# Attention tables by query tile, an own tile for the latent keys, and a Hyena front loaded and evacuated in another order

## The chip, the cores and the metric

The kernel runs on one core of a Trainium2 chip. The metric is the device time of one execution in microseconds (us). The core has a matrix engine (TensorE, PE in the profile, with its weight loads as PEld), VectorE (DVE), ScalarE (ACT), GpSimd (POOL) and SyncE (SP, which here only issues DMAs). Each engine works through its own instructions in order; semaphores tie them together. ScalarE, GpSimd and SyncE each issue DMAs from their own queue.

## The reference

Two layers of an encoder over 512 tokens of width 1024, batch 1, in float32:

```python
for layer in range(2):
    h = rms_norm(x, mix_pre_norm[layer])
    m = even_mixer(h, ...) if layer == 0 else odd_mixer(h, ...)
    x = x + rms_norm(m, mix_post_norm[layer])
    h = rms_norm(x, ffn_pre_norm[layer])
    f = (gelu(dwconv3(h @ w_gate, conv_w)) * (h @ w_up)) @ w_down      # width 2816
    x = x + rms_norm(f, ffn_post_norm[layer])
# even mixer: one projection -> 8 latent attention heads (keys of all heads share a rotated
#   part k_rope of 32) beside 8 neighbourhood heads on an 8 x 64 grid, window 8 x 16:
s = q_row . k_win * scale + rpb[:, row_off, col_off];  p = softmax(s);  o = p . v_win
# odd mixer: one projection -> 4 retention heads (q, k, v, gate) beside 512 Hyena channels:
z = dwconv3(u_proj, short_conv);  x0, x1, v = split(z);  u = v * x1
h_f, h_b = sine_mlp(t) * window                    # the filters, from 33 position features
y = irfft(rfft(u, 1024) * rfft(circ(h_f, h_b)))[:512] + u * hy_bias;  out = y * x0
# both mixers: concat of the two halves, then one output projection
```

## The kernel before, in words

Activations stand transposed: the width of 1024 as eight tiles of 128 partitions, with the 512 tokens along the free dimension. Every float32 product is made of three fp32r products (high x high, low x high, high x low), the `mm` of lines 280 to 282, so a projection of 1024 onto 128 outputs is 24 TensorE instructions with 512 columns ("128x512"). An operand is split by a ScalarE cast (the high part, line 274) and a subtraction of VectorE or GpSimd (the low part, line 275): `split_to`. Weights come as 198 pieces of 512 KB on SyncE's queue; ScalarE casts `whi` (line 259), VectorE subtracts `wlo` (line 260), and pieces are started three ahead. A scheduler in the framework orders each engine's instructions by priorities that the code sets (`high_priority`) and by fixed constraints (`issue_after`). PSUM, eight banks, is shared by tags: pj 2, A 3, B 2, C 1.

The stages, in the profile's time: norm of the input and first projections up to 50 us; neighbourhood heads, with pieces of the latent projections between them, up to about 135; latent heads up to about 250, the output projection; a boundary; the first channel mixer from about 290 to 640, and in its course the making of the Hyena filters (`filters`); a boundary; the second mixer from about 671 to 930; a boundary, and the second channel mixer.

Neighbourhood heads (`na0`, `na1`, `na2`, run in a software pipeline): 128 queries at a time look at a window of 256 keys. There are three kinds of query tile (left edge, middle, right edge). The table of relative positions `rpb` comes as one tile of 8 x 384 values per partition, in four DMAs on SyncE's queue, and the mask `namask` in another; for each head VectorE adds mask and a shifted piece of the table for each kind (line 631). The scores are scaled and biased (line 649), the largest is taken (652), ScalarE takes exponentials (660), the quotient is made (665) and turned by TensorE (671).

Latent attention: `latent_kv` makes the rotated part `kr` of the keys on VectorE and GpSimd (lines 729 to 731). `parts()`, in a later step of the pipeline, splits it three times into `kall` (three pairs of high and low parts, for three heads at a time), a tile that takes over the memory of `rpb` by the shared tag "big". The latent scores are products of `kall` with `qh` and `ql`.

A boundary ends a stage: norm, residual sum, next pre-norm. TensorE meanwhile makes four products of the next stage from the tokens before their row factor is known (`proj_halves`). The factor `rcol` is made by GpSimd (line 299), turned by TensorE (`spread`, line 316, a PSUM buffer of tag C, of which there is one) and copied by ScalarE to `Rb` (line 447); each evacuation then multiplies by it.

Second mixer: at the start ScalarE issues eight DMAs that spill x to memory, and GpSimd two for the forward transform matrices `dftfhi` and `dftflo` (line 934). `conv` evacuates four products, one after another, with the three-point convolution behind each. `spectrum` transforms the filters: their tiles `sd` are loaded by ScalarE's queue, split into `t`, and multiplied in PSUM of tag C; the first half goes to `sp` (line 1027). The signal `u` is made, turned (line 1101), transformed, multiplied by the filter's spectrum (the products `t`, split), and transformed back with `dftihi` and `dftilo`, in PSUM of tag A; the retention's token projections (`proj_tok`, giving `rv`) and three of its gates (`gate`) lie between. `decays` makes the retention's decay factors from eight numbers, 30 small instructions, before the retention.

Of the kernel before, what the change touches and what calls it, by code (L numbers as in the profile page):

```python
# [43 lines left out]
def shape_constants():  # L44
# [18 lines left out]

    mask = np.zeros((P, 3, 32, GR), np.float32)
    for typ, (q0, k0) in enumerate(((0, 0), (16, 8), (48, 32))):
        for p in range(P):
            col = q0 + p // GR
            st = min(max(col - 8, 0), GW - 16)
            kc = k0 + np.arange(32)
            mask[p, typ, (kc < st) | (kc >= st + 16), :] = -1.0e30  # L70
    c["namask"] = f32(mask.reshape(P, 3 * 256))
# [41 lines left out]
def lay_out(inp):  # L113
# [92 lines left out]
class Body:  # L206
    def __init__(self, ctx, tc, I, out, dbg=None):
# [10 lines left out]
        self.filt = self.dp.tile([2, S, HC], F32, name="filt")  # L218
        self.n = 0
        self.wi = 0  # L220
        self.wq = []
        self.cols = self.cp.tile([P, NCOL], F32, name="cols")
# [27 lines left out]
    def load_weight(self, n=1):  # L250
# [88 lines left out]
    def boundary(self, pool, tag, x, prod, gpost, gpre, ns, ftag, perm=False, rin=None):  # L339
# [218 lines left out]
    def mixer0(self, p, h, acc):  # L558
        nc = self.nc
        mask = p.tile([P, 3 * 256], F32, name="namask")  # L560
        rope = p.tile([P, 2, S], F32, name="rope0")
        big = p.tile([P, MH, 384], F32, tag="big", name="rpb")

        def loads():
            nc.sync.dma_start(mask, self.I["namask"])
            for hd in range(0, MH, 2):
                nc.sync.dma_start(big[:, hd:hd + 2], self.I["rpb"][:, hd * 384:hd * 384 + 768].rearrange("p (a b) -> p a b", a=2))
            nc.sync.dma_start(rope, self.I["rope0"].rearrange("p (a b) -> p a b", a=2))
# [53 lines left out]
        def na0(hd, _):  # L622
# [674 lines left out]
```

## Time and profile before

| | |
|---|---|
| time, median of 3 runs | 1312.72 us (1308.06, 1312.72, 1312.88) |
| profiled execution, its own time | 1307.53 us |
| its span | 1305.8 us, 16380 instructions |
| TensorE busy | 1271.7 us, 97% of the span |
| VectorE, ScalarE, GpSimd busy | 813.9, 582.9 and 80.9 us |
| granted TensorE clock, mean | 0.993 of full speed |
| DMA | 130.62 MB, mean 100 GB/s |

The profile is of one execution. A row of the timeline gives the start, the duration, the engine, the line of the kernel, the operation, output and inputs by the program's names, tile sizes, and in brackets how long the engine had been idle before and what it waited for. Matmuls are pipelined, so the spacing of their starts, not the duration of one, is the rate. In a table of stretches, "22.29 (x99)" is 22.29 us of busy time in 99 instructions, and the clock is the mean share of full speed that was granted.

### The profile page before, as it was taken

What the parts mean: (1) busy time and instruction counts of PE and PEld (TensorE: products, weight loads), DVE (VectorE), ACT (ScalarE), POOL (GpSimd) and SP (SyncE); (2) the same over time, 40 slices, a digit from 0 to 9 for tenths busy, and PEclk for the clock granted to TensorE, in tenths of its full rate; (3) what the DMA queues carried; (4) which work ended last, traced back from release to release, by engine and by line L of the source; (5) the groups of instructions that cost most, each with busy time, mean ns of one, the idle gap of its engine ahead of it and who ended that gap; (6) DMA issues with size and microseconds to landing.
All of it is one profiled execution on the core that took longest, in us unless ns stands there. A gap on an engine that the chain in (4) does not pass through costs nothing.

```text
span 1305.8 us, 16380 instructions
## 1 busy us (share of the span) xinstructions
PE 1271.7 (97%) x6370; PEld 1057.5 (81%) x6370; DVE 813.9 (62%) x1298; ACT 582.9 (45%) x943; POOL 80.9 (6%) x73
## 2 busy tenths in 40 slices
PE   9999799999999999999999999999999999999997
PEld 7788677997888788888987878778988888888886
DVE  6679898478766665322588785774875555552223
ACT  5456798456533333222454245544653333332221
POOL 4021322000000000000000000000000000000002
PEclk9999899999999999999999989999999999999999
DMA  7222012223434333333264233214233333333331
GB/s 269 86 65 79 3 33 68 82 79 116 121 123 135 122 113 97 99 111 97 83 226 128 58 120 95 81 49 130 66 113 98 97 97 97 97 97 104 107 97 65
DMA packets 41563, 130.62 MB, mean 100 GB/s; under 512 B 4652, under 2 KB 6892, under 8 KB 40973
## 3 DMA queue, kind: packets, MB, share of 16 engines
q1 hardware_dynamic: 35868, 116.92, 29.0%
q10 hardware_dynamic: 5040, 8.45, 2.0%
q0 software_dynamic: 576, 4.19, 0.9%
q8 instruction: 50, 0.82, 0.3%
q14 instruction: 29, 0.23, 0.1%
HBM read 123.26 MB, written 6.29 MB: 99 GB/s over the span
## 4 chain that ended last, share of the span: by engine, by line
PE 87%; DVE 5%; ACT 3%; issue 2%; DMA 1%; POOL 1%; SPq 0%; DVEq 0%; POOLq 0%; ACTq 0%
PE pspj L280 17%; PE pspj L282 17%; PE pspj L281 17%; PE psA L280 10%; PE psA L282 10%; PE psA L281 10%; DVE wlo L260 1%; ACT e L794 1%; DMA raw<-in_w 1%; PE psB L292 1%; PE psB L671 1%; PE psB L810 1%; DVE h L334 1%; ACT whi L259 1%; PE psC L282 1%
## 5 line engine op out<-in xcount | busy, mean ns | idle before, releaser
L259 ACT CAST whi<-raw 128x1024 fp32r<-128x1024 f32 (+1 forms) x200 | 209.1, 1048 | 432.1 <-PE pspj L281 237.8
L260 DVE TENSOR_TENSOR wlo<-raw,whi 128x1024 fp32r<-128x1024 f32 (+1 forms) x200 | 246.6, 1235 | 204.8 <-ACT whi L259 202.8
L280 PE MATMUL pspj<-h,whi 128*128 128x512 f32 (+1 forms) x664 | 250.5, 377 | 2.8 <-DVE v L599 2.7
L281 PE MATMUL pspj<-h,whi 128*128 128x512 f32 (+1 forms) x664 | 249.6, 376 | 0.0
L282 PE MATMUL pspj<-h,wlo 128*128 128x512 f32 (+1 forms) x664 | 249.4, 376 | 0.0
L282 PE MATMUL psA<-h,wlo 128*128 128x512 f32 (+1 forms) x424 | 155.4, 367 | 0.7 <-DVE wlo L260 0.7
L280 PE MATMUL psA<-h,whi 128*128 128x512 f32 (+1 forms) x424 | 156.1, 368 | 0.0
L281 PE MATMUL psA<-h,whi 128*128 128x512 f32 (+1 forms) x424 | 155.1, 366 | 0.0
L280 PEld LDWEIGHTS pspj<-h,whi 128*128 128x128 f32 x664 | 125.5, 189 | 25.4 <-DVE v L599 3.1
L282 PEld LDWEIGHTS pspj<-h,wlo 128*128 128x128 f32 x664 | 125.4, 189 | 22.2
L281 PEld LDWEIGHTS pspj<-h,whi 128*128 128x128 f32 x664 | 125.5, 189 | 22.0
L280 PE MATMUL pspj<-ahi,whi 128*128 128x512 f32 x308 | 121.4, 394 | 0.0
L282 PE MATMUL pspj<-ahi,wlo 128*128 128x512 f32 x308 | 120.7, 392 | 0.0
L281 PE MATMUL pspj<-alo,whi 128*128 128x512 f32 x308 | 119.5, 388 | 0.0
L282 PEld LDWEIGHTS psA<-h,wlo 128*128 128x128 f32 x424 | 79.8, 189 | 15.5 <-DVE wlo L260 1.9
L280 PEld LDWEIGHTS psA<-h,whi 128*128 128x128 f32 x424 | 80.0, 189 | 14.8 <-issue 2.6
L281 PEld LDWEIGHTS psA<-h,whi 128*128 128x128 f32 x424 | 80.0, 189 | 12.4
L894 DVE TENSOR_TENSOR t<-psA,Rb 128x512 f32<-128x512 f32 x40 | 27.6, 691 | 83.4 <-PE psA L282 83.3
L282 PEld LDWEIGHTS pspj<-ahi,wlo 128*128 128x128 f32 x308 | 57.8, 188 | 13.5
L281 PEld LDWEIGHTS pspj<-alo,whi 128*128 128x128 f32 x308 | 57.8, 188 | 12.9
L280 PEld LDWEIGHTS pspj<-ahi,whi 128*128 128x128 f32 x308 | 57.9, 188 | 11.5
L299 POOL TENSOR_TENSOR r<-v,mhalf 128x2 f32<-128x2 f32 (+1 forms) x14 | 13.7, 977 | 847.7 <-DVE v L297 690.2
(360 smaller groups left out, 2140.1 us busy)
## 6 DMA issues: line engine op xcount, KB each, us to landing
raw<-in_w SPq DMA_DIRECT2D x198, 512.0 KB, 3.5
x<-in_xT SPq DMA_DIRECT2D x16, 256.0 KB, 4.8
fflt<-in_fwin SPq DMA_DIRECT2D x8, 256.0 KB, 2.9
xspill<-f ACTq DMA_DIRECT2D x8, 256.0 KB, 2.6
sd<-filt ACTq DMA_DIRECT2D x8, 256.0 KB, 3.3
x<-xspill ACTq DMA_DIRECT2D x8, 256.0 KB, 3.2
rpb<-in_rpb SPq DMA_DIRECT2D x4, 384.0 KB, 4.6
filt<-fs SPq DMA_DIRECT2D x4, 256.0 KB, 2.5
```

The source lines that it names most:

```text
L259: nc.scalar.copy(hi[:, c], raw[:, c])
L260: nc.vector.tensor_tensor(lo[:, c], raw[:, c], hi[:, c].bitcast(F32), ALU.subtract)
L280: nc.tensor.matmul(ps, stat[0], mov[0], start=start, stop=False)
L281: nc.tensor.matmul(ps, stat[0], mov[1], start=False, stop=False)
L282: self.last_mm = nc.tensor.matmul(ps, stat[1], mov[0], start=False, stop=stop).ins
L292: nc.tensor.matmul(ps[:, j:j + 1], a[:, j * P:(j + 1) * P], self.ones, start=a is accs[0], stop=a is accs[-1])
L299: self.pow = nc.gpsimd.tensor_tensor(r, v, self.mhalf[:, :c], ALU.pow)
L334: self.nc.vector.scalar_tensor_tensor(lo, src, g, hi.bitcast(F32), ALU.mult, ALU.subtract)
L671: tr = lambda o, i: nc.tensor.transpose(o, i, self.ident)
L794: nc.scalar.activation(e, ps, AF.Exp, bias=nmx, accum_out=den[:, i:i + 1])
L810: nc.tensor.transpose(pt[:, i * P:(i + 1) * P], es[i][:, j * P:(j + 1) * P], self.ident)
L894: nc.vector.tensor_tensor(t, gps, Rb, ALU.mult)
```

## The change

It has these parts.

- The table of the neighbourhood heads is laid out on the host, mask included (-1e30 outside the window), as 3 x 256 values per head and partition; each head loads its 384 KB by GpSimd's queue. The mask, the big table and the additions of line 631 go. The load of `rope0` moves from SyncE's to GpSimd's queue.
- `kall` is a tile of its own, and its three splits of `kr` are made in `latent_kv`, right behind `kr`.
- `filters` splits the filters and writes high and low parts (16 DMAs of 256 KB); `spectrum` loads them as 16 pieces on GpSimd's queue, behind the transform matrices, straight into the operands. The splits of `sd` in the second mixer go.
- `decays` is made in the first channel mixer, at step 4.
- The second mixer allocates `x0` first and loads the transform matrices with a higher priority. The four products of the boundary are all scaled into `x0` first and convolved from there; the spill is issued behind the second of these convolutions' ScalarE instructions.
- `gate` and `rv` leave PSUM by a ScalarE instruction; the VectorE work follows from SBUF.
- A weight piece's cast is issued behind the copy `Rb` of the last boundary (`hold`).

```diff
--- before.py
+++ after.py
     r = np.pad(inp["a_rpb"][0], ((0, 0), (0, 0), (16, 16)))
     q = np.arange(P)
-    r = r[:, 7 - (q % GR)[:, None, None] + np.arange(GR)[None, None, :], 15 - (q // GR)[:, None, None] + np.arange(48)[None, :, None]]
-    a["rpb"] = f32(r.transpose(1, 0, 2, 3).reshape(P, MH * 384))
+    t = np.full((P, MH, 3, 32, GR), -1.0e30, np.float32)
+    for typ, (q0, k0) in enumerate(((0, 0), (16, 8), (48, 32))):
...
+        t[:, :, typ] = np.where(near[:, None, :, None], e.transpose(1, 0, 2, 3), t[:, :, typ])
+    a["rpb"] = f32(t.reshape(P, MH * 768))
...
-        self.filt = self.dp.tile([2, S, HC], F32, name="filt")
+        self.filt = self.dp.tile([2, 2, S, HC], F32, name="filt")
...
             with self.tc.high_priority(WP):
-                nc.scalar.copy(hi[:, c], raw[:, c])
+                with self.tc.issue_after(self.hold) if self.hold is not None else ExitStack():
+                    nc.scalar.copy(hi[:, c], raw[:, c])
                 nc.vector.tensor_tensor(lo[:, c], raw[:, c], hi[:, c].bitcast(F32), ALU.subtract)
...
-            nc.scalar.copy(self.Rb, self.spread(self.rcol, "C"))
+            self.hold = nc.scalar.copy(self.Rb, self.spread(self.rcol, "C")).ins
...
     def mixer0(self, p, h, acc):
-        mask = p.tile([P, 3 * 256], F32, name="namask")
         rope = p.tile([P, 2, S], F32, name="rope0")
-        big = p.tile([P, MH, 384], F32, tag="big", name="rpb")
+        kall = p.tile([P, 6, S], F32R, name="kall")
 
         def loads():
-            nc.sync.dma_start(mask, self.I["namask"])
-            for hd in range(0, MH, 2):
-                nc.sync.dma_start(big[:, hd:hd + 2], self.I["rpb"][:, hd * 384:hd * 384 + 768].rearrange("p (a b) -> p a b", a=2))
-            nc.sync.dma_start(rope, self.I["rope0"].rearrange("p (a b) -> p a b", a=2))
+            nc.gpsimd.dma_start(rope, self.I["rope0"].rearrange("p (a b) -> p a b", a=2))
...
-            b = p.tile([P, 2, 256], F32, tag="bias", bufs=2, name=self.nm("bias"))
-            b = [b[:, 0], b[:, 1], self.X("bias", tag="xb")[:, :256]]
-            for t, o in enumerate((128, 64, 0)):
-                nc.vector.tensor_tensor(b[t], big[:, hd, o:o + 256], mask[:, t * 256:t * 256 + 256], ALU.add)
-            return b
+            b = p.tile([P, 3, 256], F32, tag="bias", bufs=3, name=self.nm("bias"))
+            nc.gpsimd.dma_start(b, self.I["rpb"][:, hd * 768:hd * 768 + 768].rearrange("p (a b) -> p a b", a=3))
+            return [b[:, t] for t in range(3)]
...
-            lat["kr"] = kr
+            for i in range(3):
+                self.split_to(kall[64:128, 2 * i], kall[64:128, 2 * i + 1], kr[64:128], nc.gpsimd)
...
-            kall = p.tile([P, 6, S], F32R, tag="big", name="kall")
-            for i in range(3):
-                self.split_to(kall[64:128, 2 * i], kall[64:128, 2 * i + 1], lat["kr"][64:128], nc.gpsimd)
...
-            nc.vector.tensor_tensor(t, gps, Rb, ALU.mult)
+            scaled = nc.vector.tensor_tensor(t, gps, Rb, ALU.mult)
+            if l == 0 and j == 4:
+                with self.tc.issue_after(scaled.ins):
+                    self.decay = self.decays(self.cp)
...
             for i, src in enumerate((t, n)):
-                nc.sync.dma_start(self.filt[i, ts], src)
+                hl = self.X("fh", F32R), self.X("fl", F32R)
+                self.split_to(*hl, src)
+                for part in range(2):
+                    nc.sync.dma_start(self.filt[part, i, ts], hl[part].bitcast(F32))
...
     def spectrum(self, mats, at, kt, spec):
...
+        for m in range(4):
+            parts.append([at(m % 2) for _ in range(2)])
+            for hh in range(2):
+                tk = 2 * (m // 2) + hh
+                for part in range(2):
+                    with self.tc.high_priority(300), self.tc.issue_after(self.consts):
+                        nc.gpsimd.dma_start(parts[m][hh][part], self.filt[part, m % 2, tk * P:(tk + 1) * P])
+        yield
...
-                for hh in range(2):
-                    t = self.X("sd", tag="xb")
-                    tk = 2 * par + hh
-                    nc.scalar.dma_start(t, self.filt[trig, tk * P:(tk + 1) * P])
-                    sd.append(at(trig))
-                    self.split_to(*sd[-1], t)
...
     def mixer1(self, p, x, h, pre):
         spill = self.dp.tile([D, S], F32, name="xspill")
-        for k in range(KT):
-            nc.scalar.dma_start(spill[k * P:(k + 1) * P], x[k])
-        mats = self.dft_consts(p, "dftf")
+        x0 = [p.tile([P, S], F32, name=f"x0{j}") for j in range(4)]
+        with self.tc.high_priority(300):
+            mats = self.dft_consts(p, "dftf")
...
+        next(steps)
+        for j in range(4):
+            scaled(pre[j], x0[j])
+        u = []
         for j in range(4):
-            u.append(conv(8 + j, p.tile([P, S], F32, name=f"u{j}")))
+            u.append(conv(8 + j, p.tile([P, S], F32, name=f"u{j}"), x0[j]))
+            if j == 1:
+                with self.tc.issue_after(self.taken):
+                    for k in range(KT):
+                        nc.scalar.dma_start(spill[k * P:(k + 1) * P], x[k])
...
         def gate():
-            g, ps = self.X("rg", tag="xb"), self.proj(h)
-            nc.vector.tensor_tensor(g, ps, Rb, ALU.mult)
+            g = self.X("rg", tag="xb")
+            nc.scalar.copy(g, self.proj(h))
+            nc.vector.tensor_tensor(g, g, Rb, ALU.mult)
             nc.scalar.activation(g, g, AF.Silu)
...
         for j, ps in enumerate(self.proj_tok(h)):
+            t = self.X("rv", tag="xb")
+            nc.scalar.activation(t, ps, AF.Copy, scale=rcol[:, j:j + 1])
             rv.append(two("t1"))
-            self.scaled(rv[-1], ps, rcol[:, j:j + 1], slice(0, S))
+            self.split_to(*rv[-1], t)
...
-        lg = self.decays(p)
+        lg = self.decay
```

Lines of the changed kernel stand some two to twenty lower or higher than those of the kernel before (280 to 282 become 282 to 284, 299 becomes 301).

TensorE, second mixer, behind the last token projection; `psA_6898` is the first inverse transform before, `pspj_6826` the first gate projection of the changed kernel. Before:

```order
L280 MATMUL psA_6659<-whi_6661,h_5600 128x512
L281 MATMUL psA_6659<-wlo_6662,h_5600 128x512
L282 MATMUL psA_6659<-whi_6661,h_5601 128x512
L280 MATMUL psA_6898<-dftihi,t_1206_6550 128x256
L281 MATMUL psA_6898<-dftilo,t_1206_6550 128x256
L282 MATMUL psA_6898<-dftihi,t_1207_6551 128x256
```

And in the changed kernel, at the same place:

```order
L282 MATMUL psA_6680<-whi_6682,h_5641 128x512
L283 MATMUL psA_6680<-wlo_6683,h_5641 128x512
L284 MATMUL psA_6680<-whi_6682,h_5642 128x512
L282 MATMUL pspj_6826<-h_5627,whi_6712 128x512
L283 MATMUL pspj_6826<-h_5628,whi_6712 128x512
L284 MATMUL pspj_6826<-h_5627,wlo_6713 128x512
```

Three gate projections of 24 products each now stand ahead of the first inverse transform; before, they came behind its first head.

GpSimd, boundary ahead of the second mixer; `r` is a row factor of the post-norm, `rcol` that of the next pre-norm. Before:

```order
L299 TENSOR_TENSOR r_5564<-v_5562,mhalf 128x2
L299 TENSOR_TENSOR r_5695<-v_5693,mhalf 128x2
L934 DMA dftfhi<-in_dftf 128x2048
L299 TENSOR_TENSOR rcol_5879<-v_5982,mhalf 128x4
L934 DMA dftflo<-in_dftf 128x2048
L934 DMA dftihi<-in_dfti 128x2048
```

Changed (of the sixteen loads of filters the first three and the last two are shown, in two pieces):

```order
L301 TENSOR_TENSOR r_5736<-v_5734,mhalf 128x2
L931 DMA dftfhi<-in_dftf 128x2048
L931 DMA dftflo<-in_dftf 128x2048
L1017 DMA t_1099_6045<-filt 128x512
L1017 DMA t_1103_6053<-filt 128x512
L1017 DMA t_1100_6046<-filt 128x512
```

```order
L1017 DMA t_1110_6064<-filt 128x512
L1017 DMA t_1114_6072<-filt 128x512
L301 TENSOR_TENSOR rcol_5920<-v_6023,mhalf 128x4
L931 DMA dftihi<-in_dfti 128x2048
L931 DMA dftilo<-in_dfti 128x2048
```

All 18 loads now stand ahead of `rcol`. A load on this queue from a certain place on waits until the load eight before it has landed.

ScalarE, first mixer: the three casts of `kr` into `kall`. Before, near the end of the neighbourhood heads:

```order
L613 COPY at_1341<-psA_1332 64x512
L660 ACTIVATE s_1359,den_1351<-s_1359,nmx_1362 128x256
L274 CAST kall<-kr_718 64x512 x3
L274 CAST a_1188<-at_1341 64x512
L660 ACTIVATE ebuf_208,den_1351<-s_1359,nmx_1362 128x256
```

Changed, between two parts of an earlier head:

```order
L261 CAST whi_796<-raw_795 128x1024
L276 CAST phi_756<-psB_751 128x512
L276 CAST kall<-kr_703 64x512 x3
L656 ACTIVATE s_724,den_716<-s_724,nmx_727 128x256
L656 ACTIVATE ebuf_207,den_716<-s_724,nmx_727 128x256
```

The casts moved from a later head's exponentials to those of an earlier one.

## Rows read from the trace of the kernel before

**Rows 1.** The page's first part: busy us, share of the span, instructions.

```profile
PE 1271.7 (97%) x6370; PEld 1057.5 (81%) x6370; DVE 813.9 (62%) x1298; ACT 582.9 (45%) x943; POOL 80.9 (6%) x73
```

**Rows 2.** Stretches: length, busy time by engine, granted clock, DMA share, GB/s.

```profile
25.00:50.00 25.00, 22.29 (x99) 17.56 (x98) 12.87 (x19) 9.16 (x13) 0.57 (x1) 1.00 0.54 175
125.00:150.00 25.00, 19.80 (x98) 14.76 (x97) 20.80 (x42) 15.04 (x37) 6.25 (x5) 0.86 0.07 21
150.00:225.00 75.00, 72.17 (x363) 54.33 (x363) 66.16 (x116) 69.70 (x148) 21.07 (x16) 1.00 0.12 36
300.00:625.00 325.00, 325.00 (x1409) 262.97 (x1408) 182.46 (x259) 121.77 (x149) 0.00 (x0) 1.00 0.37 114
671.00:680.00 9.00, 6.20 (x28) 4.21 (x26) 5.25 (x16) 4.67 (x6) 2.20 (x3) 1.00 0.99 375
745.00:775.00 30.00, 26.99 (x122) 22.48 (x121) 29.97 (x48) 12.25 (x18) 1.06 (x2) 0.94 0.35 113
```

**Rows 3.** Timeline of TensorE where the latent heads begin.

```profile
139.41 0.48 PE L671 MATMUL psB<-ident,s 128*128 128x128 f32 x2 [2.99 <-DVE s L665]
...
143.62 0.63 PE L281 MATMUL psA<-kall,qh 128*128 128x512 f32 x1
...
144.05 0.63 PE L282 MATMUL psA<-kall,ql 128*128 128x512 f32 x1
...
150.51 0.40 PE L281 MATMUL psA<-kall,qh 128*128 128x512 f32 x1
...
150.74 0.40 PE L282 MATMUL psA<-kall,ql 128*128 128x512 f32 x1
```

**Rows 4.** Timeline of GpSimd and ScalarE around the second mixer's start and inverse transform.

```profile
645.50 1.08 POOL L299 TENSOR_TENSOR r<-v,mhalf 128x2 f32<-128x2 f32 x1 [8.04 <-DVE v L297]
...
670.48 0.76 POOL L934 DMA_DIRECT2D dftfhi<-in_dftf  x1 [23.91 <-ACT t L274]
...
671.52 1.40 POOL L299 TENSOR_TENSOR rcol<-v,mhalf 128x4 f32<-128x4 f32 x1 [0.28 <-DVE v L295]
...
674.78 0.57 ACT L447 COPY Rb<-psC 128x512 f32<-128x512 f32 x1
...
748.00 0.53 POOL L934 DMA_DIRECT2D dftihi<-in_dfti  x1 [74.51 <-PE psB L282]
```

**Rows 5.** Groups by line: busy us, mean ns, idle before.

```profile
L631 DVE TENSOR_TENSOR bias<-rpb,namask 128x256 f32<-128x256 f32 x24 | 10.4, 460 | 0.1
```

**Rows 6.** Timeline of GpSimd and ScalarE, neighbourhood heads.

```profile
78.14 1.29 POOL L731 TENSOR_TENSOR kr<-kr,Rb 64x512 f32<-64x512 f32 x1
...
78.83 0.51 ACT L660 ACTIVATE s<-s,nmx 128x256 f32<-128x256 f32 x1 [0.92 <-DVE nmx L652]
...
133.53 1.66 ACT L274 CAST kall<-kr 64x512 fp32r<-64x512 f32 x3
```

**Rows 7.** Timeline of TensorE in the second mixer.

```profile
676.93 0.47 PE L280 MATMUL psC<-t,dftfhi 128*128 128x512 f32 x1 [0.53 <-DMA dftfhi<-in_dftf]
...
680.10 0.50 PE L282 MATMUL psC<-t,dftflo 128*128 128x512 f32 x1 [2.24 <-DMA dftflo<-in_dftf]
...
695.73 0.50 PE L280 MATMUL psC<-t,dftfhi 128*128 128x512 f32 x1 [0.69 <-ACT sp L1027]
...
698.64 0.50 PE L1101 MATMUL psB<-ident,u 128*128 128x128 f32 x2 [1.26 <-DVE u L1090]
...
769.45 0.38 PE L280 MATMUL psA<-dftihi,t 128*128 128x256 f32 x1 [1.78 <-ACT t L274]
...
770.61 0.39 PE L282 MATMUL psA<-dftihi,t 128*128 128x256 f32 x1 [0.65 <-DVE t L275]
...
771.81 0.58 PE L282 MATMUL psA<-dftihi,t 128*128 128x256 f32 x1 [0.58 <-DVE t L275]
...
774.97 0.63 PE L281 MATMUL pspj<-h,whi 128*128 128x512 f32 x1
```

**Rows 8.** DMA issues: line's tensors, queue, count, KB each, us from issue to landing.

```profile
sd<-filt ACTq DMA_DIRECT2D x8, 256.0 KB, 3.3
```

More of the change, by code (lines that the diff above doesn't have):

```diff
@@ L194, in lay_out @@
     q = np.arange(P)
-    r = r[:, 7 - (q % GR)[:, None, None] + np.arange(GR)[None, None, :], 15 - (q // GR)[:, None, None] + np.arange(48)[None, :, None]]
-    a["rpb"] = f32(r.transpose(1, 0, 2, 3).reshape(P, MH * 384))
+    t = np.full((P, MH, 3, 32, GR), -1.0e30, np.float32)
+    for typ, (q0, k0) in enumerate(((0, 0), (16, 8), (48, 32))):
+        col, kc = q0 + q // GR, k0 + np.arange(32)
+        off = (16, 8, 0)[typ] + np.arange(32)
+        e = r[:, 7 - (q % GR)[:, None, None] + np.arange(GR)[None, None, :], 15 - (q // GR)[:, None, None] + off[None, :, None]]
+        st = np.minimum(np.maximum(col - 8, 0), GW - 16)[:, None]
+        near = (kc[None, :] >= st) & (kc[None, :] < st + 16)
+        t[:, :, typ] = np.where(near[:, None, :, None], e.transpose(1, 0, 2, 3), t[:, :, typ])
+    a["rpb"] = f32(t.reshape(P, MH * 768))
     fw = np.zeros((P, 64 + 64 + 64 + 1024), np.float32)
@@ L933, in dft_consts @@
             t = p.tile([P, 4, 2, 256], F32R, tag="dft" + part, name=name + part)
-            self.nc.gpsimd.dma_start(t.rearrange("p m a b -> p (m a b)"), self.I[name][:, i * 2048:(i + 1) * 2048])
+            self.consts = self.nc.gpsimd.dma_start(t.rearrange("p m a b -> p (m a b)"), self.I[name][:, i * 2048:(i + 1) * 2048]).ins
             out.append(t)
@@ new lines, in spectrum @@
+        parts = []
+        for m in range(4):
[6 more added lines that the diff above has]
+        yield
+        for m in range(4):
+            par, trig = m // 2, m % 2
+            sd = parts[m]
+            for ft in range(2):
+                ps = self.PS("C")
+                for hh in range(2):
+                    c = slice(ft * P, ft * P + P)
+                    self.mm(ps, (mats[0][:, m, hh, c], mats[1][:, m, hh, c]), sd[hh], hh == 0, hh == 1)
+                if par == 0:
+                    t = self.X("sp", tag="xb")
+                    nc.scalar.activation(t, ps, AF.Copy, scale=1.0 / 512)
+                    spec[ft, trig] = t
+                else:
+                    e, o, d = spec[ft, trig], kt(), kt()
+                    nc.vector.scalar_tensor_tensor(o, ps, 1.0 / 512, e, ALU.mult, ALU.add)
+                    if trig == 0:
+                        nc.vector.scalar_tensor_tensor(d, ps, -1.0 / 512, e, ALU.mult, ALU.add)
+                    else:
+                        nc.vector.scalar_tensor_tensor(d, ps, 1.0 / 512, e, ALU.mult, ALU.subtract)
+                    spec[ft, trig] = (o, d)
+                yield
@@ L1063, in mixer1, with scaled, conv @@
         spill = self.dp.tile([D, S], F32, name="xspill")
-        for k in range(KT):
-            nc.scalar.dma_start(spill[k * P:(k + 1) * P], x[k])
-        mats = self.dft_consts(p, "dftf")
+        x0 = [p.tile([P, S], F32, name=f"x0{j}") for j in range(4)]
+        with self.tc.high_priority(300):
+            mats = self.dft_consts(p, "dftf")
         two = lambda tag: tuple(p.tile([P, S], F32R, tag=tag, bufs=8, name=self.nm(tag)) for _ in range(2))
         rcol, Rb = self.rcol, self.Rb
-        def conv(jj, dst):
-            ps = pre[jj - 8] if jj >= 8 else self.proj(h, "A" if jj == 4 else "pj")
-            t = p.tile([P, S], F32, tag="cv", name=self.nm("cv"))
+        def scaled(ps, t):
             nc.vector.tensor_tensor(t, ps, Rb, ALU.mult)
+            return t
+        def conv(jj, dst, t=None):
+            if t is None:
+                t = scaled(self.proj(h, "A" if jj == 4 else "pj"), p.tile([P, S], F32, tag="cv", name=self.nm("cv")))
             cw = [self.col(C_SC + i * 12 + jj) for i in range(3)]
-            nc.scalar.activation(dst, t, AF.Copy, scale=cw[1])
+            self.taken = nc.scalar.activation(dst, t, AF.Copy, scale=cw[1]).ins
             nc.vector.scalar_tensor_tensor(dst[:, 1:], t[:, :S - 1], cw[0], dst[:, 1:], ALU.mult, ALU.add)
@@ L1084, in mixer1 @@
                               lambda: p.tile([P, S], F32, tag="t2", bufs=8, name=self.nm("ks")), ks)
-        u, x0 = [], [p.tile([P, S], F32, name=f"x0{j}") for j in range(4)]
+        next(steps)
         for j in range(4):
-            u.append(conv(8 + j, p.tile([P, S], F32, name=f"u{j}")))
+            scaled(pre[j], x0[j])
[6 more added lines that the diff above has]
+                        nc.scalar.dma_start(spill[k * P:(k + 1) * P], x[k])
         for j in range(4):
```

29 lines of the change are left out of this document (1 added, 28 removed).

## The prediction

> **What bounds the kernel now.** I read the page's first part, then a table of stretches, then the timeline of TensorE wherever a stretch of it was not full, and last the timelines of the engines that its gaps name. TensorE is busy for 97% of the span [rows 1]; no other engine comes near. The table shows that this is not even: in the first channel mixer TensorE is busy for 325.00 of 325 us, while 2.71 us are missing in 25 to 50, 5.20 in 125 to 150, 2.80 in 671 to 680 and 3.01 in 745 to 775 [rows 2]. So work taken from VectorE or ScalarE is worth nothing by itself. Only an edit that ends one of these gaps, or that lets the clock stay up behind it, moves the end. The clock is the second thing to see: in 125 to 150 the granted clock is 0.86 of full. Behind a wait of 2.99 us the 128x512 products follow each other at 0.43 us (143.62, 144.05), later at 0.23 (150.51, 150.74) [rows 2, 3]: 1.2 GHz, then 2.4. As 0.86 is a mean of the two levels, 25 x 0.14 x 2 = 7 us of that stretch were at the lower one.
>
> The number of TensorE instructions doesn't change, so the whole effect is gaps and clock. I go by gaps, in the profiled execution's own time (span 1305.8, 1307.53 in all), and count time won as positive.
>
> **Start (0 to 50): -0.5.** The rope table's load goes to GpSimd's queue, and three loads of the new table stand between the squares that GpSimd adds for the first statistics; about 2.4 MB (mask, four pieces of the table, rope) leave SyncE's queue. A GpSimd DMA issue takes 0.53 us [rows 4], so three cost up to 1.6 if each lands on the chain to the first norm. Rope's 524 KB beside the loads of x cost up to 1.4 at the 375 GB/s that the core moved when its queues were full (671 to 680) [rows 2]. Against it stands the gap of 2.71, which a regrouped start may shorten. Between -3.0 and +2.7 I take -0.5, since issues on a chain are certain and the gap's end is not.
>
> **Neighbourhood heads (50 to 125): -0.7.** The 24 additions that made the biased tables, 10.4 us of VectorE [rows 5], go; TensorE hardly waits there, so they bring nothing. The three casts of the latent key's rope half (1.66 us on ScalarE) now stand ahead of a head's exponentials. They need GpSimd's kr, which ends at 78.14 + 1.29 = 79.43, while the exponential started at 78.83 [rows 6]: it comes up to 79.43 + 1.66 - 78.83 = 2.3 us later. Weight products cover most of it; bounds -2.0 and +1.0, and I take -0.7.
>
> **Latent attention starts (125 to 150): +4.0.** In front of the transposes that waited for 2.99 us at 139.41 [rows 3], ScalarE had to do the same 1.66 us of casts (at 133.53) before the exponentials [rows 6], and VectorE up to two additions of the table, 2 x 0.46 [rows 5]. Both go: 1.7 + 0.9 = 2.6 of the 2.99. A wait cut to 0.4 us lets the clock stay, as it did behind the short waits elsewhere; seven 128x512 products stood at 0.43 instead of 0.23 (I counted them between 142.8 and 149): 1.4. Together 4.0. The upper bound is the whole gap and the clock, 5.2 + 1.4 = 6.6. The lower is 0: in the next 75 us ScalarE is busy for 69.70 [rows 2], so a head that starts earlier may wait for it later.
>
> **First channel mixer: -0.3.** Eight more casts and eight more subtractions split the filters, 16 DMAs of 256 KB go out in place of 8 of the same size, and the 30 small instructions of the retention decays come here with a change of the activation table. TensorE has no gap in 325 us, so all of it is hidden [rows 2]; uncovered, one late evacuation could cost 2.0.
>
> **Second mixer's front (670 to 703): +3.1.** Four waits are worth reading: 0.53 and 2.24 for the two halves of the transform matrix, 0.69 for ScalarE's sp, 1.26 for u [rows 7]. GpSimd issued the first half at 670.48, having waited 23.91 us, and the second only behind rcol [rows 4], although it had nothing to do from 646.58. Now both, and the 16 loads of split filters, are free to go from there, so 0.53 + 2.24 goes. The filters' own splitting (8 casts, 8 subtractions, off VectorE's way to u) goes too, and the spills are issued after it: 1.26 goes. What is late next is the row factor: all 24 products that stood on both sides of its spread now stand before it, so the first transform product, which needs the same PSUM buffer, waits for the copy Rb: 0.57 [rows 4] and some 0.3 for the hand-over, 0.9. sp stays. 0.53 + 2.24 + 1.26 - 0.9 = 3.1. Above, the 0.69 goes too and the wait costs nothing: 4.7. Below, the copy queues behind a weight cast and the four scalings of VectorE are late: -1.0.
>
> **Inverse transform (745 to 775): +5.6.** Here 1.78, 0.65 and 0.58 us were spent waiting for t, which ScalarE and VectorE split just before [rows 7]: 3.0. TensorE now does three gate projections first, 72 products of 0.23 us or 16.6 us, so t is long there. The clock had fallen: a product at 774.97 still takes 0.63, as at 144.05, where full speed shows 0.40 [rows 3, 7], and 0.94 granted over 30 us is 30 x 0.06 x 2 = 3.6 us at the lower level up to 775 [rows 2]. From there to about 778 I counted 11 of the half-size products (0.1 us dearer each) and 8 full ones (0.2): 2.6. Lower bound 3.0 (the clock falls in another place), upper 6.3. The gates' PSUM now goes by a ScalarE copy, in place of a VectorE product behind the splits; it is hidden by 24 products for each.
>
> Sum: -0.5 - 0.7 + 4.0 - 0.3 + 3.1 + 5.6 = 11.2 us, so 1296.3 on the profiled execution's time. Its 1307.53 is 5.2 under the median: two of the four executions shown lie near 1308, two near 1312.8. The same sum on the median gives 1301.5. I take the middle, 1299.
>
> **Rivals.** First, the gains at 139 and 677 are given back: ScalarE's 69.70 of 75 us sets the latent heads, and the row factor takes the place of the matrices. Then 4.1 is left of the sum (5.6 - 0.5 - 0.7 - 0.3), 7.1 less than forecast: 1306. The load of ScalarE speaks for it; against it, that load is busy time and not a wait on TensorE: 72.17 of the 75 us are full [rows 2].
>
> Second, on the other side: GpSimd's queue. rcol is made by GpSimd and now stands behind the issue of all 18 loads (6.3 MB), each of which from a certain point waits for the landing of the load eight before it: rcol can't start before ten loads, 2 x 1.05 + 8 x 0.26 = 4.2 MB, have landed. They start at 645.50 + 1.08 = 646.58. TensorE stood at the spread when rcol ended, at 671.52 + 1.40 = 672.9 [rows 4], and comes to it 12 products of 0.23 later now, near 675.7. If the queue serves one load after another at the rate of the 256 KB filter loads, 3.3 us each [rows 8], 16 of these are 52.8 us, rcol ends at 646.58 + 52.8 + 1.40 = 700.8, and TensorE waits 25.1: 1299 + 25 = 1324. It is a loss once the ten loads take over 27.7 + 11.2 = 38.9 us, that is under 108 GB/s. Against it: the two matrices, issued at 670.48 and, behind rcol, after 672.9 beside weights, were both used by 680.10 [rows 4, 7], 2.1 MB in 9.6 us or 218 GB/s, by which ten loads take 19 us. What would starve the queue is VectorE, which is busy throughout; but at 748.00 the issue of the next matrix took 0.53 us in a stretch in which VectorE was busy for 29.97 of 30 [rows 2, 4].
>
> The Trainium skill (SBUF — State Buffer, section "SBUF: two separate sides") has a rule against this part: descriptors of a DMA from GpSimd's queue can't be written while VectorE runs in a mode that takes both of a pair of ports, so that a transfer of 0.62 us took 3.1 behind a copy. By that, an estimate from its figures, ten loads would be held 10 x 2.5 = 25 us on top of the 19, and TensorE would wait 16: 1315, which I count within the chance of this rival. The trace shows no held issue at 748, but VectorE ran tensor-tensor operations there, which the page's section "Who interferes with whom" exempts; no row shows an issue beside a tensor-scalar one.
>
> Third, the start: if the three issues and the rope load cost the whole 3.0, and the head's exponentials 2.0, 3.8 of the sum goes: 1303, inside the forecast's range.
>
> **From cases to numbers.** 0.5% is 6.6 us, about what a measurement of this kernel tells from no change: faster is below 1306.1, slower above 1319.3. Forecast, with its own range of 1290 to 1306 (start included): 0.74, of which 0.04 within 0.5%. Gains given back: 0.18, half on either side of the bound. Queue late: 0.08, of which 0.06 slower. Faster 0.70 + 0.09 = 0.79, same 0.04 + 0.09 + 0.02 = 0.15, slower 0.06. The range goes from the sum with the upper bounds of the three large terms on the lower level (2.6 + 1.6 + 0.7 more), the start's (3.2 more) and the lower of the two levels (2.6 from the middle), 1288, to the first rival on the upper level, 1308.6, and 1.4 for a part of the start, 1310; what lies outside is mostly the queue.
>
> **What would show it.** Right: no wait over 1 us before the transposes near 139 and a granted clock near 1.00 from 125 to 150; GpSimd's 18 issues between 646 and 671; no DMA named before the forward transform, but about 0.9 us for Rb; gate products before the inverse transform, and no wait for t. Wrong: rcol's start later than 674 with TensorE waiting at the spread; a clock under 0.9 in another place; TensorE waiting for exponentials between 150 and 225 by as much as was won before.

## The result and the profile after

The changed kernel took 1298.11 us (median of 4 runs, 1295.68 to 1300.66) against 1312.10 of the kernel before; the ratio of the two is 0.990, with a 95% interval of 0.9866 to 0.9933. 1299 was forecast. Two executions lie near 1295.7 us, with a mean granted clock of 0.996, and two near 1300.5, with 0.992, so that the median, like the forecast, stands between them. The profiled execution has a span of 1294.0 us, 11.8 less than before; the forecast's sum was 11.2.

To see whether the sum is right for the forecast's reasons, I added up by stage how much later each TensorE product ended after the one before it than the usual spacing of its form (0.227 us for 128x512, for example). This "TensorE loss" holds idle time, restarts (the first product after a wait ends late) and a fallen clock. It is read from one execution of each kernel. Where kernels have the same order of instructions, it agrees within 0.1 us in the stretches 75 to 100, 100 to 125 and 650 to 725, but only within 1.8 in the start (7.3 to 9.1) and 0.9 in 125 to 150 (6.5 to 7.4). Times of the stages are those of the kernel before:

| stage, us | loss before | changed | gain | forecast |
|---|---|---|---|---|
| start, 0 to 50 | 7.4 | 7.5 | -0.1 | -0.5 |
| neighbourhood heads, 50 to 125 | 2.8 | 6.4 | -3.5 | -0.7 |
| latent heads begin, 125 to 150 | 10.6 | 7.4 | +3.2 | +4.0 |
| latent heads, 150 to 300 | 9.7 | 9.4 | +0.3 | 0 |
| first channel mixer, 300 to 650 | 3.1 | 3.2 | -0.1 | -0.3 |
| second mixer's front, 650 to 725 | 8.2 | 3.1 | +5.2 | +3.1 |
| inverse transform, 725 to 800 | 7.0 | 0.3 | +6.7 | +5.6 |
| the rest | 9.5 | 9.2 | +0.3 | 0 |

The total agrees because errors of both signs cancel: the second mixer won 3.2 us more than forecast, and the neighbourhood heads lost 2.8 more. That the total came out so close is luck; that all six terms have the right sign is not. Three of the six terms lie outside the bounds that the forecast gave them: the heads (-3.5, lowest -2.0), the second mixer's front (+5.2, highest +4.7) and the inverse transform (+6.7, highest +6.3). The stretches of the changed kernel that answer to [rows 2] (same columns):

```profile
75.00:100.00 25.00, 23.08 (x128) 19.04 (x129) 19.25 (x34) 13.99 (x33) 9.76 (x8) 1.00 0.25 73
100.00:125.00 25.00, 24.29 (x138) 20.04 (x137) 18.43 (x43) 14.82 (x35) 4.34 (x4) 1.00 0.27 80
125.00:150.00 25.00, 22.65 (x111) 16.56 (x111) 22.85 (x44) 15.48 (x39) 4.26 (x3) 0.93 0.14 43
...
671.00:680.00 9.00, 8.32 (x39) 6.66 (x38) 5.07 (x10) 3.82 (x5) 1.03 (x1) 1.00 0.65 205
745.00:775.00 30.00, 30.00 (x134) 24.86 (x133) 29.24 (x44) 18.07 (x27) 0.00 (x0) 1.00 0.42 137
```

From 745 to 775 TensorE is full and the clock is at its upper level. From 125 to 150 the gap shrank from 5.20 to 2.35 us, but the clock still fell (0.93, was 0.86). And 1.92 us are now missing in 75 to 100 and 0.71 in 100 to 125. The kernel before had no gap there:

```profile
75.00:100.00 25.00, 25.00 (x140) 21.07 (x140) 22.24 (x45) 13.79 (x32) 5.05 (x4) 1.00 0.18 53
100.00:125.00 25.00, 25.00 (x143) 21.16 (x142) 22.19 (x46) 15.92 (x37) 5.29 (x4) 1.00 0.24 75
```

The timeline of the changed kernel, ScalarE and TensorE, says why (it answers to [rows 3, 6, 7]):

```profile
79.24 1.66 ACT L276 CAST kall<-kr 64x512 fp32r<-64x512 f32 x3 [1.38 <-POOL kr L727]
...
80.93 0.51 ACT L656 ACTIVATE s<-s,nmx 128x256 f32<-128x256 f32 x1
...
83.31 0.39 PE L582 MATMUL psA<-phi,v 128*128 128x256 f32 x1 [1.32 <-ACT phi L276]
...
86.63 0.39 PE L583 MATMUL psA<-plo,v 128*128 128x256 f32 x1 [0.60 <-DVE plo L277]
...
117.28 0.65 PE L318 MATMUL psC<-ident,r 128*128 128x128 f32 x4 [0.71 <-POOL r L301]
...
139.09 0.50 PE L282 MATMUL pspj<-lh,whi 128*128 128x512 f32 x1 [1.50 <-DVE qf L772]
...
676.70 0.50 PE L282 MATMUL psC<-t,dftfhi 128*128 128x512 f32 x1 [0.68 <-ACT Rb L449]
```

ScalarE waits 1.38 us for GpSimd's kr, casts for 1.66, and the exponential that started at 78.83 before [rows 6] starts at 80.93. What follows from it, the operand phi, is late: by 83.31 TensorE has stood for 1.32 us. At 117.28 it stands for a row factor r. At 139.09 a projection waits 1.50 us until VectorE has emptied a PSUM buffer into qf; the forecast had only the wait at the transposes near there, cut to 0.4 us. At 676.70 there is no DMA in the bracket any more; the copy Rb is there, with 0.68 us.

GpSimd's queue, on which the slower rival rested (it answers to [rows 4]):

```profile
646.56 0.60 POOL L931 DMA_DIRECT2D dftfhi<-in_dftf  x1
...
652.87 0.53 POOL L1017 DMA_DIRECT2D t<-filt  x1 [1.98 <-DMA dftfhi<-in_dftf]
...
662.38 1.05 POOL L1017 DMA_DIRECT2D t<-filt  x2 [1.18 <-DMA t<-filt]
671.53 1.03 POOL L301 TENSOR_TENSOR rcol<-v,mhalf 128x4 f32<-128x4 f32 x1 [8.10 <-DVE nlg L1198]
```

The ninth issue, at 652.87, waited for the landing of the first load, eight before it. The last of the 18 ended at 663.43 (662.38 + 1.05), and GpSimd was idle for 8.10 us before rcol. The queue was nowhere near the path.

### The profile page after: what moved, and what is told of

Read it like the earlier page. It is cut to its first block, busy times and chain, and to the rows that moved or that the text cites. A ratio compares the mean times of both kernels' runs of the same rounds, so it can differ in the third digit from the quotient of the medians.

```text
span 1294.0 us, 16446 instructions
## 1 busy us (share of the span) xinstructions
PE 1266.1 (98%) x6370; PEld 1052.7 (81%) x6370; DVE 805.7 (62%) x1274; ACT 587.9 (45%) x951; POOL 92.6 (7%) x98
## 4 chain that ended last, share of the span: by engine, by line
PE 85%; ACT 3%; DVE 2%; issue 2%; POOL 1%; DMA 0%; POOLq 0%; DVEq 0%; ACTq 0%
PE pspj L282 16%; PE pspj L284 16%; PE pspj L283 16%; PE psA L282 10%; PE psA L284 10%; PE psA L283 10%; ACT e L788 1%; PE psB L294 1%; PE psB L804 1%; PE psC L282 1%; PE psC L283 1%; POOL r L301 1%; PE psC L284 1%; ACT whi L261 1%; DVE wlo L262 0%
```

## The experiments

**One part alone: gates.** The kernel before, with the gates and `rv` leaving PSUM by ScalarE.

```diff
-            g, ps = self.X("rg", tag="xb"), self.proj(h)
-            nc.vector.tensor_tensor(g, ps, Rb, ALU.mult)
+            g = self.X("rg", tag="xb")
+            nc.scalar.copy(g, self.proj(h))
+            nc.vector.tensor_tensor(g, g, Rb, ALU.mult)
...
```

> The kernel before with one part of the change alone: the gates and rv leave PSUM by ScalarE. In this kernel three gate projections stand ahead of the first inverse-transform product, as in the changed kernel. My theory (the order of TensorE hides the splits of t, and the clock stays): the waits of 1.78, 0.65 and 0.58 us before the inverse transform vanish, the granted clock from 745 to 800 us is 1.00 in place of 0.94, and the run is 6 to 6.6 us shorter than the kernel before, with nothing else changed. Rival (it is the work taken off VectorE and ScalarE in the second mixer, the filters' splits and the decays, that makes t early): the waits for t stay above 1 us in sum and the gain is under 2 us.

It took 1304.35 us against 1309.90, ratio 0.9957 (0.9941 to 0.9974): 5.6 us less, just short of the 6 to 6.6 expected. Its stretches around the inverse transform:

```profile
745.00:775.00 30.00, 30.00 (x134) 24.85 (x133) 29.96 (x48) 12.99 (x20) 1.06 (x2) 1.00 0.32 106
775.00:800.00 25.00, 25.00 (x157) 22.66 (x156) 17.75 (x24) 12.96 (x18) 0.00 (x0) 1.00 0.45 139
```

No gap, full clock, and VectorE as busy as before (29.96 of 30). VectorE doesn't make t earlier either: two of its subtractions for t start at 771.60 and 772.81, before at 769.87 and 771.07, which is the 1.7 us by which this execution already runs later at 652. So it is the order of TensorE that hides them; the rival falls.

**One part alone: matrices.** The kernel before, with `x0` allocated first and the transform matrices loaded with a higher priority.

```diff
-        mats = self.dft_consts(p, "dftf")
+        x0 = [p.tile([P, S], F32, name=f"x0{j}") for j in range(4)]
+        with self.tc.high_priority(300):
+            mats = self.dft_consts(p, "dftf")
...
```

> The kernel before with only the transform matrices allocated behind x0 and loaded with a higher priority. Theory: both loads start at about 646.6, the waits of 0.53 and 2.24 us for them go, and a wait for the row factor's copy Rb of about 0.7 us appears, since in this kernel too the spread stands behind all of the boundary's 24 psA products; gain 2.0 to 2.6 us, and the wait for u (1.26 us) stays. Rival (DMA supply: 671 to 680 was full at 375 GB/s, and the early loads only push the filter loads and weights): the gain is under 1 us, with a wait for a filter load or a weight piece in its place.

1303.53 against 1309.90 us, ratio 0.9960 (0.9947 to 0.9974). That is 6.4 us, and 2.0 to 2.6 were expected. The loss from 650 to 725 fell by 2.4 us, from 8.2 to 5.9. Another 1.8 lie in the inverse transform, where this kernel's order is that of before. TensorE waits there as before, 3.4 us in four waits, but the clock stayed up, and 4.8 us were lost from 745 to 800 in place of 6.6:

```profile
745.00:775.00 30.00, 26.53 (x124) 21.61 (x123) 29.96 (x47) 12.32 (x18) 1.13 (x2) 1.00 0.37 123
775.00:800.00 25.00, 25.00 (x147) 22.17 (x146) 14.10 (x19) 8.24 (x11) 0.00 (x0) 1.00 0.30 96
```

The other 2.2 us are no difference of the two profiles, whose spans differ by 4.2; where they come from isn't shown. TensorE's waits from 668 to 703 (us in total, times, longest):

```profile
PE psB L1103 <- DVE u L1092: 1.3, 1, 1.3
PE psC L280 <- ACT Rb L447: 1.0, 1, 1.0
PE psC L280 <- ACT sp L1027: 0.7, 1, 0.7
```

The waits of 0.53 and 2.24 for the matrices [rows 7] are gone, 1.0 for the copy Rb is new, and u stays: the waits are the forecast's working of this part, line by line, though the time is not.

**The casts of kr, two ways.** First the high parts on GpSimd, so that ScalarE needn't wait:

```diff
-                self.split_to(kall[64:128, 2 * i], kall[64:128, 2 * i + 1], kr[64:128], nc.gpsimd)
+                hi = kall[64:128, 2 * i]
+                nc.gpsimd.tensor_copy(hi, kr[64:128])
+                nc.gpsimd.tensor_tensor(kall[64:128, 2 * i + 1], kr[64:128], hi.bitcast(F32), ALU.subtract)
```

> The changed kernel with the high parts of the latent key's rope half made on GpSimd too, so that ScalarE does not wait for kr in front of a head's exponentials. Theory (these casts, 1.38 us of wait and 1.66 of work, delayed the exponentials by 2.1 us, and TensorE paid for it at 83.3 and 86.6): the waits of 1.32 us for phi and 0.60 for plo go, and the TensorE time lost between 75 and 100 us falls from 3.3 to about 1.0, 2.3 us less; total 1.5 to 2.5 us shorter than the changed kernel. Rival (the heads are late for another reason, the table's loads or the order of TensorE): no change within 0.5 us.

1295.50 us; ratio to before 0.9906 (0.9879 to 0.9932). Its four runs (1293.40 to 1300.13) overlap with those of the changed kernel, so the time alone doesn't tell the two apart; the stretch does. The stretch, and GpSimd's rows:

```profile
75.00:100.00 25.00, 25.00 (x139) 21.02 (x138) 22.22 (x37) 12.82 (x31) 11.98 (x11) 1.00 0.24 74
```

```profile
80.85 1.17 POOL L730 CAST kall<-kr 64x512 fp32r<-64x512 f32 x2
81.98 3.56 POOL L731 TENSOR_TENSOR kall<-kr,kall 64x512 fp32r<-64x512 f32 x2
```

TensorE is full again, and the loss there is 0.8, not 3.3: the casts were the cause. Second, the casts held back to about 118 to 130 us:

```diff
+                with self.tc.issue_after(self.at):
+                    nc.scalar.copy(kall[64:128, 2 * i], lat["kr"][64:128])
...
```

> The changed kernel with the three casts of kr held back until a ScalarE copy of a late neighbourhood head (about 118 to 130 us), one at a time between other work, in place of 79 us. Theory: the loss between 75 and 100 us falls from 3.3 to about 1.0; the part of the gain at 139 that came from taking 1.66 us of casts away from there is given back, so the wait there grows by 0 to 1.7 us; sum between 0 and 2.3 us shorter than the changed kernel. Rival (the gain at 139 came from the additions of the table that are gone, and the casts are harmless there): the full 2.3 us is kept. A second rival: the casts matter at 139 more than at 79, and the run is longer than the changed kernel.

1298.79 us, the time of the changed kernel. The loss from 75 to 100 is 0.8 here too, but from 125 to 150 it is 9.1 in place of 7.4. Behind the casts, which now stand from 124.59 to 127.78, TensorE has two waits that the changed kernel lacks:

```profile
130.03 0.39 PE L582 MATMUL psA<-phi,v 128*128 128x256 f32 x1 [0.87 <-ACT phi L276]
...
133.52 0.38 PE L283 MATMUL psA<-qkl,qkh 64*128 64x256 f32 x1 [1.03 <-DVE qkl L277]
```

So up to 1.8 us of the gain of 3.2 in this stage came from moving the casts away; part of the 1.8 is the clock (0.86 here, 0.93 in the changed kernel). The 1.5 that are left may be the table's additions, but no run has the additions alone. The forecast had put 1.7 on the casts and 0.9 on the additions.

**Without the hold.** The changed kernel without the constraint on weight casts.

```diff
-            self.hold = nc.scalar.copy(self.Rb, self.spread(self.rcol, "C")).ins
+            self.hold2 = nc.scalar.copy(self.Rb, self.spread(self.rcol, "C")).ins
```

> The changed kernel without the constraint that holds a weight piece's cast behind the copy of the row factor. ScalarE's order then has two casts of weight pieces (1.05 us each, of pieces that land late) ahead of the copy Rb in the second mixer's boundary. Theory (since all 24 boundary products stand ahead of the spread, the copy is now on TensorE's path): the wait for Rb before the first transform product grows from 0.68 us to 2.8 or more, 2 to 5 us longer than the changed kernel. Rival (ScalarE is idle there anyway, as it was before the change): the wait stays under 1 us and the time is the same.

1304.96 us, ratio to before 0.9949 (0.9931 to 0.9968), 6.8 above the changed kernel's 1298.11. ScalarE and TensorE:

```profile
680.07 1.04 ACT L261 CAST whi<-raw 128x1024 fp32r<-128x1024 f32 x1 [2.69 <-DMA raw<-in_w]
681.02 0.58 ACT L449 COPY Rb<-psC 128x512 f32<-128x512 f32 x1
...
681.66 0.79 PE L282 MATMUL psC<-t,dftfhi 128*128 128x512 f32 x1 [5.53 <-ACT Rb L449]
682.25 0.63 PE L283 MATMUL psC<-t,dftfhi 128*128 128x512 f32 x1
682.67 0.63 PE L284 MATMUL psC<-t,dftflo 128*128 128x512 f32 x1
```

The copy stood behind a cast that waited for its weight piece, and TensorE waited 5.53 us. Behind that wait seven products come 0.43 us apart (1.2 GHz, the lower level of the clock), which adds 1.4 us. The theory's cause holds; its range of 2 to 5 us doesn't.

**Convolutions as before.** Each product scaled just ahead of its convolution, the spill at the start.

```diff
-        for j in range(4):
-            scaled(pre[j], x0[j])
+        for k in range(KT):
+            nc.scalar.dma_start(spill[k * P:(k + 1) * P], x[k])
...
-            u.append(conv(8 + j, p.tile([P, S], F32, name=f"u{j}"), x0[j]))
...
+            u.append(conv(8 + j, p.tile([P, S], F32, name=f"u{j}"), scaled(pre[j], x0[j])))
```

> The changed kernel with the four boundary products scaled one by one, each followed by its convolution, and the spill of x issued at the stage's start, as in the kernel before. Theory (the second mixer's front won 5.1 us of TensorE time, of which the matrices alone gave 2.3; the rest, 2.8, is the filters' splits that are gone and the order of the convolutions): the wait for u comes back in part, 0.5 to 1.5 us between 675 and 703, and no more. Rival 1 (the order of the evacuations is what removed the wait for u): the wait for u returns with its full 1.3 us and the restart. Rival 2 (it was the filters' splits alone): no change, under 0.3 us.

1298.95 us. The loss from 675 to 700 is 2.23, against 1.86: this part is worth 0.4 us. A wait of 0.8 for a scaled product stands where sp had 0.5; the one for u did not come back. 0.4 lies between rival 2 (under 0.3) and the theory (0.5 to 1.5); rival 1 falls.

**Late loads.** The third experiment's kernel, with rope and all tables held back behind the first row factor.

```diff
+            with self.tc.issue_after(pow0):
+                nc.gpsimd.dma_start(b, self.I["rpb"][:, hd * 768:hd * 768 + 768].rearrange("p (a b) -> p a b", a=3))
...
```

> The third experiment's kernel (latent key's high parts on GpSimd) with the rope load and all table loads held back behind GpSimd's making of the first row factor. Theory (at the start, 10 to 20 us, the changed kernel moved 304 GB/s against 234, and the weight pieces came late: waits of 1.7 to 2.0 us for a weight's low part and 1.7 for rcol): the loss in 0 to 50 us falls from 8.9 in the third experiment to 6.5 to 7.5; total 1 to 2 us shorter. Rival (these waits come from x and the weights' own landing, not from rope and tables): the loss in 0 to 50 stays within 0.7 of 8.9. A second rival: the tables arrive late for head 0, with a wait for bias after 50 us.

1293.44 us; the loss from 0 to 50 is 7.0, inside the theory's 6.5 to 7.5. Then the statistics earlier as well:

```diff
+            with self.tc.high_priority(HP):
+                self.stats([acc], D, out=self.rcol)
...
```

> As the run before it, with the first row factor's statistics given a higher priority, so that VectorE does v ahead of a weight piece's subtraction (in the changed kernel it stands behind it, in the kernel before ahead). Theory: the wait of TensorE for rcol near 29 us, 1.7 us, falls to under 0.5, total another 1 to 1.5 us shorter. Rival: the statistics' products now stand 17 products earlier on TensorE and wait there for the last squares of GpSimd, so the wait only moves: within 0.5 us of the run before it, or longer.

1295.82 us, 2.4 more: the wait moved to the statistics' products, as the rival had it:

```profile
20.31 0.83 PE L294 MATMUL psB<-ones,sq 128*128 128x1 f32 x6 [3.96 <-POOL sq L546]
```

**Filters split late.** The changed kernel with whole filters, loaded by ScalarE's queue and split in the second mixer.

```diff
+            for hh in range(2):
+                t = self.X("sd", tag="xb")
+                nc.scalar.dma_start(t, self.filt[trig, tk * P:(tk + 1) * P])
+                sd.append(at(trig))
+                self.split_to(*sd[-1], t)
...
```

> The changed kernel with the filters written and loaded unsplit, by ScalarE's queue, and split in the second mixer by ScalarE and VectorE, as in the kernel before; everything else is the changed kernel's. Theory (the front won 5.1 us of TensorE time; the matrices alone gave 2.3 and the order of the convolutions 0.4, so the filters' splits account for the rest): the TensorE loss from 650 to 703 rises from 3.0 to about 5.4, with waits for u or sp, and the run is about 2.4 us longer than the changed kernel. Rival (the rest was the row factor's copy and chance): under 1 us longer.

1305.57 us, 7.4 above the changed kernel on the same chip; the loss from 650 to 725 is 8.0, against 3.1. From its timeline, ScalarE's queue, ScalarE and TensorE:

```profile
692.21 0.81 ACTq L1014 DMA_DIRECT2D sd<-filt  x2
...
696.73 0.62 ACT L276 CAST t<-sd 128x512 fp32r<-128x512 f32 x1 [3.93 <-DMA sd<-filt]
...
697.40 0.80 PE L282 MATMUL psC<-t,dftfhi 128*128 128x512 f32 x1 [3.67 <-ACT t L276]
```

The direction is the theory's, the cause is not: what TensorE paid for is a load issued at 692.21 (in ScalarE's order behind its other work of this stage), for which the cast waited 3.93 us, and not the splitting, of which a cast took 0.62. So what the splitting itself costs there isn't shown.

**Filter loads by ScalarE.** The 16 loads of split filters on ScalarE's queue.

```diff
-                        nc.gpsimd.dma_start(parts[m][hh][part], self.filt[part, m % 2, tk * P:(tk + 1) * P])
+                        nc.scalar.dma_start(parts[m][hh][part].bitcast(F32), self.filt[part, m % 2, tk * P:(tk + 1) * P])
```

> The changed kernel with the 16 loads of split filters issued by ScalarE in place of GpSimd. ScalarE's order then has all 16 issues, of 0.4 to 0.5 us each, ahead of a weight cast and the row factor's copy. Theory (GpSimd's queue costs nothing here, since it was done 8 us before rcol; ScalarE's stands on the path): 2 to 7 us longer than the changed kernel, with a wait for Rb or a weight piece near 677. Rival (loads on GpSimd's queue are held by VectorE, as the rule on the shared port has it, and ScalarE's are not): the same time or shorter.

1304.62 us, 6.5 above the changed kernel. The same engines in this kernel's timeline:

```profile
670.49 2.39 ACTq L1017 DMA_DIRECT2D t<-filt  x5
...
677.13 1.29 ACTq L1017 DMA_DIRECT2D t<-filt  x3
...
682.50 1.04 ACT L261 CAST whi<-raw 128x1024 fp32r<-128x1024 f32 x1 [11.27 <-DMA t<-filt]
683.45 0.58 ACT L449 COPY Rb<-psC 128x512 f32<-128x512 f32 x1
...
684.08 0.80 PE L282 MATMUL psC<-t,dftfhi 128*128 128x512 f32 x1 [6.77 <-ACT Rb L449]
```

The issues stopped for 4.25 us from 672.88 on (670.49 + 2.39), and a cast and the copy Rb stood behind them on ScalarE: TensorE waited 6.77 us for Rb, in the changed kernel 0.68. What these issues waited for was not another load of the filters. The one at 677.13 came right behind the landing, at 677.11, of a weight piece that SyncE had issued at 671.57. The next stop, before 679.66, was for SyncE's next piece, as the profile's chain of releases has it (start, us, what):

```profile
672.70 6.94 DMA raw<-in_w
679.66 0.33 ACTq L1017
```

An issue took ScalarE 0.44 us (median) and GpSimd, in the changed kernel, 0.53; GpSimd's issues stopped too (at most 2 us), but in time that it had. The Trainium skill (SBUF — State Buffer, "SBUF: two separate sides") says that GpSimd can't write the descriptors of its DMAs while VectorE runs an operation in a two-port mode. No run here tests that: while GpSimd issued, from 646 to 664, VectorE was busy for 18.00 of 18 us, but with tensor-tensor and scalar-tensor-tensor operations alone.

**A faster kernel.** Last the changed kernel and the seventh experiment side by side:

> The changed kernel once more, beside the next run on the same chip. Expected: 1298 us within 2, and the TensorE loss by stage as in its first profile, but for the start (0 to 50 us), which differed by up to 1.8 us between runs whose order of instructions there is the same.

> The seventh experiment's kernel again, beside the changed kernel. Theory (2.5 us from the heads near 80, and little or nothing from the start): 2 to 4 us shorter than the changed kernel on the same chip, with an interval that leaves zero out. Rival (the heads' gain is given back by the clock near 140, where the seventh run lost 1.7 us more than the third): within 1 us of it.

The changed kernel took 1298.17 us (6 runs, 1296.76 to 1301.25), as expected, the other 1295.01 (6 runs, 1292.08 to 1295.93): 3.2 us less, with no overlap; ratios to before 0.9908 (0.9876 to 0.9939) and 0.9874 (0.9840 to 0.9908). The start lost 7.3 to 9.1 us in eight profiles with the changed kernel's order, 7.0 and 6.5 in the two with late loads alone. So some 1.6 us are won there, but the stretch from 125 to 150 gives as much back, in both profiles (loss 8.8, where the third experiment had 7.1), with a clock of 0.86. Both profiles are of executions near the upper end of their kernel's runs (1294.58 and 1295.64), so it isn't shown that every execution loses this. Two stretches of the last kernel:

```profile
75.00:100.00 25.00, 25.00 (x141) 20.92 (x140) 22.62 (x40) 13.97 (x33) 13.47 (x12) 1.00 0.31 95
...
125.00:150.00 25.00, 22.64 (x104) 16.17 (x102) 21.48 (x44) 15.34 (x40) 4.56 (x4) 0.86 0.07 22
```

Why the clock falls longer there when TensorE is as busy as in the changed kernel (22.64 and 22.65 us) stays open. Late loads alone don't bring it: the eighth experiment's kernel has them too, and its clock stayed at 1.00 there, with a loss of 6.9.

## Why the prediction came out, step by step

- **Inverse transform, +5.6:** right in place, cause and size (6.7 in its stage; alone, from 745 to 800, 6.6). Missing in the sum were the restarts: a first product after a wait ends some 0.27 us later than the usual spacing, three times. The 2.6 for the clock hold for the profiled execution. In that of the second experiment, with much the same waits, the clock stayed up and 1.8 us less were lost.
- **Second mixer's front, +3.1:** the matrices' part came as worked out. 5.2 was measured: the waits that the forecast names gave 3.6, and 1.6 are restarts (1.3) and small gaps that it left out. Which part removed the wait for u isn't separated: it is absent without the new order of the convolutions (sixth experiment) and with the splits back (ninth). Two things were costed too low in what they protect: the hold (wait of 5.53 without it; my lower bound had one cast in mind, not a piece that had yet to land) and the filters' early loads (3.67). The parts don't add up: without the hold this stage loses 8.9 us, more than before the change (8.2), though every other part is in place.
- **Latent heads begin, +4.0:** 3.2. The casts' share is confirmed by holding them back; the additions' share is what remains, and no run tests it. Two of the forecast's own signs did not come: TensorE still waits 1.50 us at 139.09, for qf, which was not in the sum, and only half of the clock came back (0.93, not 1.00). Of the six profiles with the changed kernel's order there, four show 0.93 and two 1.00; the two lost 6.5 and 6.8, which would be gains of 4.1 and 3.8.
- **Neighbourhood heads, -0.7: the step that failed.** That the exponentials come 2 us later was right (2.10). "Weight products cover most of it" was wrong: the stretch lost 2.3 us more from 75 to 100. Another 1.3 were lost from 100 to 125, of which 0.9 at the row factor of 117.28. Between its statistics and its spread TensorE has 0.7 us of other products, before 1.6. This loss stayed in every kernel with the new tables, and the forecast had no term for it.
- **Start, -0.5:** -0.4 on the means (three profiles with the old order lost 7.9, eight with the new 8.4), within what one start differs from the next. That the moved loads cost something is shown by holding them back (7.0 and 6.5).
- **The rivals:** GpSimd's queue was done 8 us early. The gains were not given back between 150 and 225 (loss 8.6 and 8.3), whatever ScalarE's load.

## What to carry to other kernels

On a path bound by one engine, look for the gaps and what ends them, and give that engine other work there: an order that put 72 products ahead of a wait won 6.6 us alone, 1.8 of it by a clock that doesn't fall in every execution. Before a step is moved earlier on a helper, see what waits for that helper in the next 2 to 5 us; three casts, 1.66 us on a ScalarE that was busy for 14 of 25 us, cost TensorE 2.3. And once a single PSUM buffer's copy stands on the path, everything ahead of it on its engine has that price: 5.5 us for weight casts, 6.8 for DMA issues.

## What the runs showed of the hardware

- A run of load issues on one engine's queue can stop until a load from another queue has landed, and holds all that stands behind it on that engine: 4.25 us on ScalarE, for a weight piece of SyncE.
- A cast of 64x512 took GpSimd 0.58 to 0.67 us (1.17 for two), a subtraction of the same size 1.31 to 1.78 (3.56 for two).
- Behind TensorE's waits of 5.53 and 6.77 us the next products came 0.43 us apart, the lower level of the clock. Behind the wait of 2.24 us in the kernel before, at 680.10, they came at the upper level. Behind much the same three or four short waits before the inverse transform the clock fell in one execution (0.94 from 745 to 775) and stayed up in another (1.00).
